# Hybrid decoder trunk: the first projection loaded and used two k at a time, the last output quarter in column halves

## The chip, the cores and the metric
The kernel runs on one core of one Trainium2 chip. The metric is the device time of one launch in microseconds (us). Three runs of the kernel before took 1369.51, 1371.07 and 1371.03 us; the median is 1371.03.

## What is computed
The reference is a four-layer decoder trunk on an input of 256 tokens by 1024 features, all float32. Layers 0 and 3 mix tokens by retention, layer 1 by block-sparse attention, layer 2 by differential attention; each layer ends with a squared-ReLU MLP.

```python
for i in range(DEPTH):                       # 4 layers
    h = _rmsnorm(x, norm1[i])
    m = mixer(h)                             # i % 3: retention, MoBA, differential
    x = x + m
    x = x + _squared_relu_mlp(_rmsnorm(x, norm2[i]), w_up[i], w_down[i])

def _retention_mixer(h, w_in, w_out):        # 4 heads, keys of 256, values of 512
    q, k, v, g = split(h @ w_in)
    q = _rotary(q);  k = _rotary(k) * dk ** -0.5
    s_in = (q @ k.T) * inner_decay
    ...                                      # s_in @ v, normed, gated by silu(g), @ w_out
```

## The kernel before
Every large matrix product is made of float32 parts split in two: a value is rounded to `hi` (ScalarE copies it into the type fp32r) and the rest is `lo` (VectorE subtracts). Three matmuls make one product (`passes`, L296 to L299): hi x hi (L297), hi x lo (L298) and lo x hi (L299). The labels in the trace sort the operand names; for the query and key projections L299 is the matmul that reads `wlo`.

Weights are streamed through three 1 MB buffers `raw`, filled by SP's DMA queue in the order of the list `specs`. Each `raw` is cut into two pieces. For each piece ScalarE writes `whi` (L164) and VectorE writes `wlo` (L174). `advance` (L179) issues these splits up to four pieces ahead of the piece in use, `take` hands a piece to the matmuls, and when the second piece of a buffer has been split, the DMA that refills the buffer is issued (`load_raw`, L134).

The schedule is written out by hand: every engine executes its instructions in the order in which the program issues them. `later(n, fn)` puts a step off by n ticks, and `tick()`, called between groups of matmuls, issues what is due.

The beginning. SP loads x in four blocks of 256 KB with the first weights in between (L202 to L211). ScalarE's queue loads the identity matrix `ident` and the norm weights `rows`, POOL's the small tables (L213 to L220). `norm_quarter` (L266) turns x: two TensorE transposes into one PSUM bank (L272), two ScalarE operations that scale by the norm weight and write `xhi` (L275), two VectorE operations that write `xlo` (L278). The first half of the features (k = 0 to 3) is turned before the first matmul, and the first piece of weights is split; the second half is turned at the first tick, after the matmuls of k = 0 to 2 (`mm_a`, L301, with `first_of_phase`). `rms` (due at tick 3) computes the row norms with two ScalarE squares over x (L284), a POOL operation and VectorE's reciprocal (L289). The row norm itself is applied later, to results.

In `retention`, head 0 makes its query part (w = 0) and its key part (w = 1), each with 48 matmuls of 256 columns into one bank, two pieces each. After each, `rotary` (L417) runs four VectorE operations that read the bank and the cosine table `kd` (L413). Then come the value and gate projections with 512 columns (`vg`).

The end. `finish` (L348) closes the last MLP product by quarters of x, with nine matmuls of 512 columns for each: VectorE scales the bank and adds it to x (L362) and SP stores the quarter (L364).

Of the kernel before, what the change touches and what calls it, by code (L numbers as in the profile page):

```python
# [16 lines left out]
P = 128  # L17
# [14 lines left out]
def trunk(ctx, tc, x_in, rel_bias, norm1, norm2, w_up, w_down, ret_w_in, ret_w_out,  # L32
# [24 lines left out]
    def aux_bank(name):  # L57
        return pa.tile([P, 512], F32, tag="aux", name=name)
# [7 lines left out]
    def later(n, fn, *a):  # L66
        clock[1] += 1
        pending.append((clock[0] + n, ORDER.get(fn.__name__, 3), clock[1], fn, a))
# [62 lines left out]
    raws, pieces = {}, {}  # L131
    nxt = [0, 0, 0, 0]

    def load_raw(half=None):  # L134
        i = nxt[0]
        if i >= len(specs):
            return
        src, a, b = specs[i]
        if half != 1:
            raws[i] = rp.tile([P, a, b], F32, tag="raw", name="raw", bufs=NRAW)  # L140
        if half is None:
            nc.sync.dma_start(raws[i], src)
        else:
            hs = slice(half * (a // 2), (half + 1) * (a // 2))
            nc.sync.dma_start(raws[i][:, hs, :], src[:, hs, :])
        if half != 0:
            nxt[0] += 1

    def parts(i, n):
        m = n if i else n // 2  # L150
        return [slice(c, c + m) for c in range(0, n, m)]

    def split_piece():
        i = nxt[1]
        r = i // 2
        if r >= len(specs):
            return
        nxt[1] += 1
        _, a, b = specs[r]
        half = raws[r][:, (i % 2) * (a // 2):(i % 2 + 1) * (a // 2), :]  # L160
        hi = wp.tile([P, a // 2, b], F32R, tag="hi", name="whi", bufs=NPC)
        lo = wp.tile([P, a // 2, b], F32R, tag="lo", name="wlo", bufs=NPC)
        for part in parts(i, a // 2):
            ACT.activation(hi[:, part], half[:, part], AF.Copy)  # L164
        pieces[i] = (hi, lo, half)
# [31 lines left out]
    X = const.tile([P, 2, D], F32, name="X")  # L197
    xf = x_in.rearrange("b s d -> (b s) d")
    warm = const.tile([P, 1], F32, name="warm")
    DVE.memset(warm, 0.0)  # L200
    ACT.dma_start(ident, c_ident)
    nc.sync.dma_start(X[:, 0, 0:512], xf[0:P, 0:512])  # L202
    ACT.dma_start(rows, norm1.rearrange("l (c p) -> (l c) p", p=P))
    nc.sync.dma_start(X[:, 1, 0:512], xf[P:S, 0:512])
    ACT.activation(warm, warm, AF.Copy)
    load_raw(0)
    for t in range(2):
        nc.sync.dma_start(X[:, t, 512:D], xf[t * P:(t + 1) * P, 512:D])
    load_raw(1)
    for _ in range(1, NRAW):  # L210
        load_raw()  # L211
    rb = const.tile([NB_REL, AH], F32, name="rb")
    POOL.dma_start(rb, rel_bias)  # L213
    rows2 = mp.tile([64, P], F32, tag="t2k", name="rows2", bufs=4)
    POOL.memset(rows2, 0.0)
    POOL.dma_start(rows2[0:32, :], norm2.rearrange("l (c p) -> (l c) p", p=P))
    for i, w in enumerate((moba_q_norm, moba_k_norm, diff_q_norm, diff_k_norm)):
        for g in range(2):
            POOL.dma_start(rows2[32 + i:33 + i, g * HD:(g + 1) * HD], w)
    POOL.dma_start(rows2[36:37, :], diff_subln)  # L220

    W = const.tile([P, 96], F32, name="W")
    wps = aux_bank("wps")
# [21 lines left out]
    def rsqrt(y, v, name, eng):  # L245
        t = small(name + "_t", list(v.shape))
        eng.tensor_scalar(y.bitcast(I32), v.bitcast(I32), -0.5, 1597463007.0, op0=OP.mult, op1=OP.add)
        for _ in range(3):
# [4 lines left out]
            else:  # L253
                eng.tensor_tensor(t, t, v, op=OP.mult)
                eng.tensor_scalar(t, t, -0.5, 1.5, op0=OP.mult, op1=OP.add)
                eng.tensor_tensor(y, t, y, op=OP.mult)

    junk = const.tile([P, D], mybir.dt.bfloat16, name="junk")

    st = {}  # L260

# [4 lines left out]
    def norm_quarter(l, which, c, t):  # L266
        tt = slice(t * P, (t + 1) * P)
        for pair in range(2):
            ps = aux_bank("xt")
            for i in range(2):  # L270
                k = c * 4 + pair * 2 + i
                PE.transpose(ps[:, i * P:(i + 1) * P], X[:, t, k * P:(k + 1) * P], ident)  # L272
            for i in range(2):
                k = c * 4 + pair * 2 + i
                ACT.activation(st["hi"][:, k, tt], ps[:, i * P:(i + 1) * P], AF.Copy, scale=wn(l, which, k))  # L275
            for i in range(2):
                k = c * 4 + pair * 2 + i
                DVE.scalar_tensor_tensor(st["lo"][:, k, tt], ps[:, i * P:(i + 1) * P], wn(l, which, k),  # L278
                                         st["hi"][:, k, tt].bitcast(F32), op0=OP.mult, op1=OP.subtract)
# [21 lines left out]
    def mm_a(ps, half, first_of_phase=False):  # L301
        if not first_of_phase:
            advance()
        hi, lo = take()
        for m in range(2):
            for kk in range(4):
                k = half * 4 + kk
                passes(ps[:, m * S:(m + 1) * S], hi[:, kk, m * P:(m + 1) * P], lo[:, kk, m * P:(m + 1) * P],
                       st["hi"][:, k, :], st["lo"][:, k, :],
                       half == 0 and m == 0 and kk == 0, half == 1 and m == 1 and kk == 3)  # L310
                if first_of_phase and m == 0 and kk == 2:
                    tick()
        tick()

    def mm_b(pst, q, first_of_phase=False):
        if not first_of_phase:
            advance()
        hi, lo = take()
        for kk in range(2):
            k = q * 2 + kk  # L320
            for t in range(2):
                tt = slice(t * P, (t + 1) * P)
                passes(pst[t], st["hi"][:, k, tt], st["lo"][:, k, tt], hi[:, kk, :], lo[:, kk, :],
                       q == 0 and kk == 0, q == 3 and kk == 1)
            if first_of_phase and kk == 0:
                tick()
# [14 lines left out]
    def out_piece(src, first):  # L341
# [3 lines left out]
            mm_o(q, pc, src, first, False)  # L345
        tick()

    def finish(srcs, r2, nxt_norm):  # L348
        advance(4, 4)
        pcs = [take() for _ in srcs]  # L350
        if nxt_norm is not None:
            norm_new()
        for q in QUARTERS:
            for i, (pc, src) in enumerate(zip(pcs, srcs)):
                mm_o(q, pc, src, False, i == len(srcs) - 1)
            c, t = q
            xs = X[:, t, c * 512:(c + 1) * 512]
            ps = st["acc"][q]
            if r2 is None:
                DVE.tensor_tensor(xs, ps, xs, op=OP.add)  # L360
            else:
                DVE.scalar_tensor_tensor(xs, ps, r2[:, t:t + 1], xs, op0=OP.mult, op1=OP.add)  # L362
            if nxt_norm is None:
                nc.sync.dma_start(out.rearrange("b s d -> (b s) d")[t * P:(t + 1) * P, c * 512:(c + 1) * 512], xs)  # L364
            else:
                later(2, norm_quarter, nxt_norm[0], nxt_norm[1], c, t)
            tick()
        if nxt_norm is not None:
            later(3, rms, nxt_norm[1])
# [39 lines left out]

    def retention(l):  # L410
        OT = {}
        kd = mp.tile([P, 8, S], F32, tag="kd", name="kd")
        ACT.dma_start(kd[:, 0:6, :], c_rd.rearrange("a p s -> p a s"))  # L413
        cos_b = kd[:, 0:1, :].to_broadcast([P, 2, S])
        sin_b = kd[:, 1:2, :].to_broadcast([P, 2, S])

# [71 lines left out]
        for h in range(RH):  # L488
            e = {}
            qk = up_.tile([P, 4, S], F32, tag="p4k", name="qk", bufs=6)  # L490
            e["qk"] = qk
            for w in range(2):
                ps = aux_bank("qk")
                mm_a(ps, 0, h == 0 and w == 0)
                mm_a(ps, 1)
                rotary(ps, qk[:, 2 * w:2 * w + 2, :])
            later(2, scores, h, e)
            for w in range(2):
                pst = [mm_bank("vg") for _ in range(2)]
                for q in range(4):  # L500
                    mm_b(pst, q)
                    tick()
                if w == 0:
                    vh = up_.tile([P, 2, 512], F32R, tag="p4k", name="vh", bufs=6)
                    vl = up_.tile([P, 2, 512], F32R, tag="p4k", name="vl", bufs=6)
                    for t in range(2):
                        ACT.activation(vh[:, t, :], pst[t], AF.Copy)
                    for t in range(2):
                        DVE.tensor_tensor(vl[:, t, :], pst[t], vh[:, t, :].bitcast(F32), op=OP.subtract)
                    e["v"] = vh, vl  # L510
                    later(1, av, h, e)
                else:
                    gate(h, e, pst)
                    for t in range(2):
                        gated(h, e, t)
                        later(2, to_feat, h, e, t)
# [237 lines left out]


    norm_new()
    for t in range(2):
        norm_quarter(0, 0, 0, t)
    split_piece()
    split_lo()  # L760
    for t in range(2):
        later(1, norm_quarter, 0, 0, 1, t)
    later(1, split_piece)
    later(1, split_lo)
    later(3, rms, 0)
    later(10, head_weights)
    for l in range(DEPTH):
        if l % 3 == 0:
            retention(l)
# [46 lines left out]
```

## Time and profile before
| | |
|---|---|
| runs | 1369.51, 1371.07, 1371.03 us |
| profiled execution | 1369.67 us |
| its span, first to last instruction | 1367.9 us |
| VectorE, ScalarE, POOL busy | 840.8 us (61%), 689.7 us (50%), 107.1 us (8%) |
| moved by DMA | 242.27 MB, mean 177 GB/s |

Of the 40 equal slices of the span the first and the last have the array less than fully busy:

```profile
PE   7999999999999999999999999999999999999998
```

One slice is 34.2 us. Each digit is the busy share in tenths. The profile's clock line shows full speed in all slices, also where the spacing of the matmuls at the very start shows half of it; so the spacing is the better witness there.

### The profile page before, as it was taken

To read this page: it belongs to the slowest core of one execution; us is meant where nothing else is said; L and a number is where in the kernel's file an instruction comes from. 1 tells how busy PE (TensorE), PEld (TensorE's weight loads), DVE (VectorE), ACT (ScalarE), POOL (GpSimd) and SP (SyncE) were. 2 spreads that over 40 slices of the span, in tenths; PEclk is the share of its full clock that TensorE was granted. 3 is DMA by queue.
4 is the path that set the end of the run, shared out by engine and by line. 5 is a ranking of instruction groups with operands and counts; after the bars stand their busy time and mean duration, and the time that the engine had idled before them with its cause. 6 is when DMAs were issued, how large, how long until landed. Compare 5 with 4: busy or idle time off the path is not lost.

```text
span 1367.9 us, 19806 instructions
## 1 busy us (share of the span) xinstructions
PE 1351.8 (99%) x8020; PEld 1188.7 (87%) x8020; DVE 840.8 (61%) x1238; ACT 689.7 (50%) x1063; POOL 107.1 (8%) x314
## 2 busy tenths in 40 slices
PE   7999999999999999999999999999999999999998
PEld 7888889999987779999987789999988888899997
DVE  6766647555568856555578675555667675555554
ACT  5554436444456745444466754444454444544442
POOL 3111100000032000000021200000031011000000
PEclk9999999999999999999999999999999999999999
DMA  8545464555565346555554346555564555465551
GB/s 274 184 155 184 156 214 157 187 187 188 193 206 181 123 124 219 185 185 185 184 172 137 124 154 216 185 185 185 176 206 144 174 185 185 154 215 186 185 184 63
DMA packets 140797, 242.27 MB, mean 177 GB/s; under 512 B 4256, under 2 KB 87920, under 8 KB 140704
## 3 DMA queue, kind: packets, MB, share of 16 engines
q1 hardware_dynamic: 137872, 236.99, 51.5%
q0 software_dynamic: 1072, 2.35, 0.6%
q10 hardware_dynamic: 1760, 1.66, 0.4%
q8 instruction: 63, 1.03, 0.3%
q14 instruction: 30, 0.25, 0.1%
HBM read 239.91 MB, written 1.07 MB: 176 GB/s over the span
## 4 chain that ended last, share of the span: by engine, by line
PE 97%; ACT 1%; DMA 0%; DVE 0%; issue 0%; SPq 0%; ACTq 0%; DVEq 0%
PE acc L297 12%; PE acc L298 12%; PE acc L299 12%; PE up L299 9%; PE up L298 9%; PE up L297 9%; PE vg L297 4%; PE vg L299 4%; PE vg L298 4%; PE qkv L297 3%; PE qkv L299 3%; PE qkv L298 3%; PE qk L299 2%; PE qk L297 2%; PE qk L298 2%; PE xt L272 1%
## 5 line engine op out<-in xcount | busy, mean ns | idle before, releaser
L174 DVE TENSOR_TENSOR wlo<-raw,whi 128x1024 fp32r<-128x1024 f32 (+1 forms) x449 | 529.5, 1219 | 108.1 <-ACT whi L164 105.8
L164 ACT ACTIVATE whi<-raw 128x1024 fp32r<-128x1024 f32 (+1 forms) x449 | 451.9, 1051 | 90.8 <-PE acc L299 66.8
L297 PE MATMUL up<-xhi,whi 128*128 128x256 f32 x1024 | 290.1, 283 | 0.0
L299 PE MATMUL up<-xhi,wlo 128*128 128x256 f32 x1024 | 289.8, 283 | 0.0
L298 PE MATMUL up<-xlo,whi 128*128 128x256 f32 x1024 | 289.7, 283 | 0.0
L297 PE MATMUL acc<-whi,uu 128*128 128x512 f32 x512 | 200.5, 392 | 0.0
L298 PE MATMUL acc<-wlo,uu 128*128 128x512 f32 x512 | 199.9, 390 | 0.0
L299 PE MATMUL acc<-whi,uu 128*128 128x512 f32 x512 | 199.3, 389 | 0.0
L298 PEld LDWEIGHTS up<-xlo,whi 128*128 128x128 f32 x1024 | 196.3, 192 | 2.2
L297 PEld LDWEIGHTS up<-xhi,whi 128*128 128x128 f32 x1024 | 196.3, 192 | 2.2
L299 PEld LDWEIGHTS up<-xhi,wlo 128*128 128x128 f32 x1024 | 196.3, 192 | 0.0
L378 DVE SCALAR_TENSOR_TENSOR u<-up,u 128x512 f32<-128x512 f32 x64 | 44.2, 691 | 221.7 <-ACT u L377 221.5
L377 ACT ACTIVATE u<-up 128x512 f32<-128x512 f32 x64 | 38.1, 596 | 258.9 <-PE up L299 258.9
L299 PEld LDWEIGHTS acc<-whi,uu 128*128 128x128 f32 x512 | 96.1, 188 | 20.5
L297 PEld LDWEIGHTS acc<-whi,uu 128*128 128x128 f32 x512 | 96.4, 188 | 18.2
L298 PEld LDWEIGHTS acc<-wlo,uu 128*128 128x128 f32 x512 | 96.4, 188 | 17.6
L297 PE MATMUL vg<-whi,xhi 128*128 128x512 f32 x256 | 100.6, 393 | 0.0
L299 PE MATMUL vg<-whi,xlo 128*128 128x512 f32 x256 | 99.8, 390 | 0.0
L298 PE MATMUL vg<-wlo,xhi 128*128 128x512 f32 x256 | 99.7, 390 | 0.0
L297 PE MATMUL qkv<-whi,xhi 128*128 128x512 f32 x192 | 78.0, 406 | 0.0
L297 PE MATMUL acc<-whi,oh 128*128 128x512 f32 x192 | 76.4, 398 | 0.0
L297 PE MATMUL qk<-xhi,whi 128*128 128x256 f32 x256 | 74.0, 289 | 1.8 <-ACT whi L164 1.8
(212 smaller groups left out, 1807.7 us busy)
## 6 DMA issues: line engine op xcount, KB each, us to landing
raw<-in_w_up_dram SPq DMA_DIRECT2D x64, 1024.0 KB, 5.5
raw<-in_w_down_dram SPq DMA_DIRECT2D x64, 1024.0 KB, 5.9
raw<-in_ret_w_in_dram SPq DMA_DIRECT2D x47, 1024.0 KB, 5.2
raw<-in_ret_w_out_dram SPq DMA_DIRECT2D x16, 1024.0 KB, 4.9
raw<-in_moba_w_in_dram SPq DMA_DIRECT2D x12, 1024.0 KB, 5.2
raw<-in_diff_w_in_dram SPq DMA_DIRECT2D x12, 1024.0 KB, 5.1
raw<-in_moba_w_out_dram SPq DMA_DIRECT2D x4, 1024.0 KB, 4.8
raw<-in_diff_w_out_dram SPq DMA_DIRECT2D x4, 1024.0 KB, 4.7
```

The lines of the kernel that those rows point to most:

```text
L164: ACT.activation(hi[:, part], half[:, part], AF.Copy)
L174: DVE.tensor_tensor(lo[:, part], half[:, part], hi[:, part].bitcast(F32), op=OP.subtract)
L272: PE.transpose(ps[:, i * P:(i + 1) * P], X[:, t, k * P:(k + 1) * P], ident)
L297: PE.matmul(ps, lhsT=ah, rhs=bh, start=first, stop=False, skip_group_check=True)
L298: PE.matmul(ps, lhsT=ah, rhs=bl, start=False, stop=False, skip_group_check=True)
L299: PE.matmul(ps, lhsT=al, rhs=bh, start=False, stop=last, skip_group_check=True)
L377: ACT.activation(u, ps, AF.Relu)
L378: DVE.scalar_tensor_tensor(u, ps, 0.0, u, op0=OP.max, op1=OP.mult)
```

## The change
At the beginning, `load_raw` takes a part number, so that a 1 MB weight buffer is loaded in quarters (two k each) or halves. x is loaded in column blocks of 256, in turn with the quarters of the first weights; its first block comes half from SP's queue and half from ScalarE's. The cosine table of layer 0 (`kd0`) comes on SP's queue in two parts. Nine matmuls of bf16 zeros (`hot`) are issued on TensorE ahead of everything else, on a tile that VectorE sets to zero first. A new function `first_qk` makes the query part of head 0: `arrive(pr)` turns two k of x and splits two k of weights, and is called for the next pair after the matmuls of each even k. `rms` comes due at its third tick (k = 7). Pieces 2 and 3 are split in two steps each, as only piece 0 was. POOL's small loads move to tick 4, the head weights to tick 14.

At the end, `last_quarter` makes the last quarter as two blocks of 256 columns, each with its own matmuls, VectorE operation and store.

```diff
-    def load_raw(half=None):
+    def load_raw(part=0, of=1):
...
+        hs = slice(part * (a // of), (part + 1) * (a // of))
+        nc.sync.dma_start(raws[i][:, hs, :], src[:, hs, :])
+        if part == of - 1:
             nxt[0] += 1
...
     def parts(i, n):
-        m = n if i else n // 2
+        m = n if i > 3 else n // 2
...
+    junk = const.tile([P, D], mybir.dt.bfloat16, name="junk")
+    kd0 = mp.tile([P, 8, S], F32, tag="kd", name="kd")
+    DVE.memset(junk, 0.0)
     DVE.memset(warm, 0.0)
+    nc.sync.dma_start(X[:, 0, 0:S], xf[0:P, 0:S])
     ACT.dma_start(ident, c_ident)
+    load_raw(0, 4)
+    ACT.dma_start(X[:, 1, 0:S], xf[P:S, 0:S])
     ACT.dma_start(rows, norm1.rearrange("l (c p) -> (l c) p", p=P))
     ACT.activation(warm, warm, AF.Copy)
+    for i in range(1, 4):
+        nc.sync.dma_start(X[:, :, i * S:(i + 1) * S], xv[:, :, i * S:(i + 1) * S])
+        load_raw(i, 4)
+    load_raw(0, 2)
+    nc.sync.dma_start(kd0[:, 0:2, :], rd[:, 0:2, :])
+    load_raw(1, 2)
+    for i in range(2):
+        load_raw(i, 2)
+    nc.sync.dma_start(kd0[:, 2:6, :], rd[:, 2:6, :])
+    hot = aux_bank("hot")
+    for _ in range(9):
+        PE.matmul(hot, lhsT=junk[:, :P], rhs=junk[:, :512], start=True, stop=True)
...
+    def first_qk(ps):
...
+        def arrive(pr):
+            bank = aux_bank("xt")
+            for i in range(2):
+                for t in range(2):
+                    c0 = i * S + t * P
+                    k = 2 * pr + i
+                    PE.transpose(bank[:, c0:c0 + P], X[:, t, k * P:(k + 1) * P], ident)
+            for i in range(2):
+                k = 2 * pr + i
+                ACT.activation(st["hi"][:, k, :], bank[:, i * S:(i + 1) * S], AF.Copy, scale=wn(0, 0, k))
+            for i in range(2):
+                k = 2 * pr + i
+                DVE.scalar_tensor_tensor(st["lo"][:, k, :], bank[:, i * S:(i + 1) * S], wn(0, 0, k),
+                                         st["hi"][:, k, :].bitcast(F32), op0=OP.mult, op1=OP.subtract)
+            hi, lo = pieces[pr // 2]
+            kk = slice(pr % 2 * 2, pr % 2 * 2 + 2)
+            raw = raws[0][:, 2 * pr:2 * pr + 2, :]
+            ACT.activation(hi[:, kk], raw, AF.Copy)
+            DVE.tensor_tensor(lo[:, kk], raw, hi[:, kk].bitcast(F32), op=OP.subtract)
+
+        arrive(0)
+        for k in range(KC):
...
+            for m in range(2):
+                mc = slice(m * P, (m + 1) * P)
+                passes(ps[:, m * S:(m + 1) * S], hi[:, kk, mc], lo[:, kk, mc], st["hi"][:, k, :], st["lo"][:, k, :],
+                       k == 0 and m == 0, k == KC - 1 and m == 1)
+            if k % 2 == 0 and k < KC - 2:
+                arrive(k // 2 + 1)
+            if k in (3, 5, 7):
+                tick()
+        nxt[1] = nxt[2] = nxt[3] = 2
...
+        load_raw()
...
+    def last_quarter(pcs, srcs, r2):
+        for e in range(2):
+            cc = slice(512 + e * S, 512 + (e + 1) * S)
+            ps = st["acc"][1, 1][:, e * S:(e + 1) * S]
+            for i, ((hi, lo), (uh, ul)) in enumerate(zip(pcs, srcs)):
+                passes(ps, uh[:, P:S], ul[:, P:S], hi[:, 0, cc], lo[:, 0, cc], False, e == 1 and i == len(srcs) - 1)
+            xs = X[:, 1, cc]
+            DVE.scalar_tensor_tensor(xs, ps, r2[:, 1:2], xs, op0=OP.mult, op1=OP.add)
+            nc.sync.dma_start(out.rearrange("b s d -> (b s) d")[P:S, cc], xs)
...
-                mm_a(ps, 0, h == 0 and w == 0)
-                mm_a(ps, 1)
+                if l == 0 and h == 0 and w == 0:
+                    first_qk(ps)
+                else:
+                    mm_a(ps, 0, h == 0 and w == 0)
+                    mm_a(ps, 1)
...
-    for t in range(2):
-        norm_quarter(0, 0, 0, t)
-    split_piece()
-    split_lo()
-    for t in range(2):
-        later(1, norm_quarter, 0, 0, 1, t)
-    later(1, split_piece)
-    later(1, split_lo)
     later(3, rms, 0)
-    later(10, head_weights)
+    later(4, small_loads)
+    later(14, head_weights)
```

## Rows read from the trace of the kernel before

**Rows 1.** Page, part 1: engine, busy time, share of the span, instructions.
```profile
PE 1351.8 (99%) x8020; PEld 1188.7 (87%) x8020; DVE 840.8 (61%) x1238; ACT 689.7 (50%) x1063; POOL 107.1 (8%) x314
```

**Rows 2.** Timeline, TensorE, 8.8 to 20 us: start, length, engine, line, operation.
```profile
8.89 0.58 PE L297 MATMUL qk<-xhi,whi 128*128 128x256 f32 x1 [1.83 <-ACT whi L164]
...
9.99 0.42 PE L297 MATMUL qk<-xhi,whi 128*128 128x256 f32 x1
10.21 0.42 PE L298 MATMUL qk<-xlo,whi 128*128 128x256 f32 x1
...
15.04 0.30 PE L297 MATMUL qk<-xhi,whi 128*128 128x256 f32 x1
...
15.41 0.28 PE L297 MATMUL qk<-xhi,whi 128*128 128x256 f32 x1
...
16.88 0.39 PE L299 MATMUL qk<-xhi,wlo 128*128 128x256 f32 x1 [0.36 <-DVE wlo L174]
17.11 0.28 PE L297 MATMUL qk<-xhi,whi 128*128 128x256 f32 x1
...
19.85 0.28 PE L299 MATMUL qk<-xhi,wlo 128*128 128x256 f32 x1
```

**Rows 3.** Timeline, ScalarE, 5.8 to 9 us.
```profile
5.81 0.63 ACT L275 ACTIVATE xhi<-xt,W 128x128 fp32r<-128x128 f32 x2 [2.65 <-PE xt L272]
...
8.21 0.63 ACT L164 ACTIVATE whi<-raw 128x512 fp32r<-128x512 f32 x1 [0.22 <-DMA raw<-in_ret_w_in_dram]
...
8.74 0.62 ACT L164 ACTIVATE whi<-raw 128x512 fp32r<-128x512 f32 x1
```

**Rows 4.** Timeline, VectorE, 0 to 10 us.
```profile
0.81 0.06 DVE L200 MEMSET warm<- 128x1 f32 x1 [0.81 <-PEq L804]
...
6.47 0.35 DVE L278 SCALAR_TENSOR_TENSOR xlo<-xt,W,xhi 128x128 fp32r<-128x128 f32 x1 [1.09 <-ACT xhi L275]
...
8.87 1.29 DVE L174 TENSOR_TENSOR wlo<-raw,whi 128x512 fp32r<-128x512 f32 x2 [0.23 <-ACT whi L164]
```

**Rows 5.** Timeline, ScalarE and VectorE, 21 to 26.1 us: row norm, then rotary.
```profile
21.33 1.05 ACT L284 ACTIVATE junk<-X 128x1024 bf16<-128x1024 f32 x1
...
23.97 0.17 DVE L289 RECIPROCAL r<-me 128x2 f32<-128x2 f32 x1 [1.09 <-POOL me L286]
24.05 0.69 DVE L421 TENSOR_TENSOR ra<-qk,kd 128x512 f32<-128x512 f32 x1
...
26.05 2.36 DVE L174 TENSOR_TENSOR wlo<-raw,whi 128x1024 fp32r<-128x1024 f32 x2
```

**Rows 6.** Timelines at 774 and 777 us; last row by line: duration ns min/median/max.
```profile
774.10 0.84 ACT L734 ACTIVATE oh<-oT,qsc 128x256 fp32r<-128x256 f32 x2
...
777.12 0.87 DVE L735 SCALAR_TENSOR_TENSOR ol<-oT,qsc,oh 128x256 fp32r<-128x256 f32 x2
...
L735 DVE SCALAR_TENSOR_TENSOR ol<-oT,qsc,oh x8: 476/478/484, 777.1 to 794.8; 128x256 fp32r<-128x256 f32 x8
```

**Rows 7.** Timeline, 56.6 to 57.5 us: transposes and ScalarE's read of them.
```profile
56.81 0.93 PE L481 MATMUL oT<-ident,go 128*128 128x128 f32 x7
57.44 0.60 ACT L485 ACTIVATE oh<-oT 128x512 fp32r<-128x512 f32 x1 [2.37 <-PE oT L481]
```

**Rows 8.** DMA issues, first 40 us: count, KB each, median us to landing.
```profile
raw<-in_ret_w_in_dram SPq DMA_DIRECT2D x2, 512.0 KB, 7.5
...
rows<-in_norm_dram ACTq DMA_DIRECT2D x1, 16.0 KB, 3.5
```

**Rows 9.** Timelines from 1363 us; last row: busy times of a stretch, GB/s last.
```profile
1363.01 0.39 PE L298 MATMUL acc<-wlo,uu 128*128 128x512 f32 x1
1363.23 0.39 PE L299 MATMUL acc<-whi,uu 128*128 128x512 f32 x1
...
1363.66 0.75 DVE L362 SCALAR_TENSOR_TENSOR X<-acc,r,X 128x512 f32<-128x512 f32 x1 [1.29 <-PE acc L299]
...
1365.40:1366.10 0.70, 0.00 (x0) 0.00 (x0) 0.00 (x0) 0.00 (x0) 0.00 (x0) 1.00 0.82 310
```

More of the change, by code (lines that the diff above doesn't have):

```diff
@@ L138, in load_raw @@
         src, a, b = specs[i]
-        if half != 1:
+        if part == 0:
             raws[i] = rp.tile([P, a, b], F32, tag="raw", name="raw", bufs=NRAW)
[L141 to L146, printed above, removed]
+        hs = slice(part * (a // of), (part + 1) * (a // of))
+        nc.sync.dma_start(raws[i][:, hs, :], src[:, hs, :])
+        if part == of - 1:
             nxt[0] += 1
     def parts(i, n):
-        m = n if i else n // 2
+        m = n if i > 3 else n // 2
         return [slice(c, c + m) for c in range(0, n, m)]
@@ L199, in trunk, with small_loads @@
     warm = const.tile([P, 1], F32, name="warm")
+    junk = const.tile([P, D], mybir.dt.bfloat16, name="junk")
+    kd0 = mp.tile([P, 8, S], F32, tag="kd", name="kd")
+    rd = c_rd.rearrange("a p s -> p a s")
+    DVE.memset(junk, 0.0)
     DVE.memset(warm, 0.0)
+    xv = xf.rearrange("(t p) d -> p t d", p=P)
+    nc.sync.dma_start(X[:, 0, 0:S], xf[0:P, 0:S])
     ACT.dma_start(ident, c_ident)
-    nc.sync.dma_start(X[:, 0, 0:512], xf[0:P, 0:512])
+    load_raw(0, 4)
+    ACT.dma_start(X[:, 1, 0:S], xf[P:S, 0:S])
     ACT.dma_start(rows, norm1.rearrange("l (c p) -> (l c) p", p=P))
-    nc.sync.dma_start(X[:, 1, 0:512], xf[P:S, 0:512])
     ACT.activation(warm, warm, AF.Copy)
-    load_raw(0)
-    for t in range(2):
[L208 to L211, printed above, removed]
+    for i in range(1, 4):
[10 more added lines that the diff above has]
+        PE.matmul(hot, lhsT=junk[:, :P], rhs=junk[:, :512], start=True, stop=True)
     rb = const.tile([NB_REL, AH], F32, name="rb")
-    POOL.dma_start(rb, rel_bias)
     rows2 = mp.tile([64, P], F32, tag="t2k", name="rows2", bufs=4)
[L215 to L220, printed above, removed]
+    def small_loads():
+        POOL.dma_start(rb, rel_bias)
+        POOL.memset(rows2, 0.0)
+        POOL.dma_start(rows2[0:32, :], norm2.rearrange("l (c p) -> (l c) p", p=P))
+        for i, w in enumerate((moba_q_norm, moba_k_norm, diff_q_norm, diff_k_norm)):
+            for g in range(2):
+                POOL.dma_start(rows2[32 + i:33 + i, g * HD:(g + 1) * HD], w)
+        POOL.dma_start(rows2[36:37, :], diff_subln)
     W = const.tile([P, 96], F32, name="W")
@@ L256, in rsqrt @@
                 eng.tensor_tensor(y, t, y, op=OP.mult)
-    junk = const.tile([P, D], mybir.dt.bfloat16, name="junk")
     st = {}
@@ L313, in mm_a @@
         tick()
+    def first_qk(ps):
+        for i in range(2):
+            hi = wp.tile([P, 4, S], F32R, tag="hi", name="whi", bufs=NPC)
+            lo = wp.tile([P, 4, S], F32R, tag="lo", name="wlo", bufs=NPC)
+            pieces[i] = (hi, lo)
+        def arrive(pr):
[8 more added lines that the diff above has]
+                ACT.activation(st["hi"][:, k, :], bank[:, i * S:(i + 1) * S], AF.Copy, scale=wn(0, 0, k))
+            for i in range(2):
+                k = 2 * pr + i
[8 more added lines that the diff above has]
+        for k in range(KC):
+            hi, lo = pieces[k // 4]
+            kk = k % 4
+            for m in range(2):
[7 more added lines that the diff above has]
+        nxt[1] = nxt[2] = nxt[3] = 2
+        for i in range(2):
+            pieces.pop(i)
+        load_raw()
     def mm_b(pst, q, first_of_phase=False):
@@ L353, in finish @@
         for q in QUARTERS:
+            c, t = q
+            if nxt_norm is None and q == QUARTERS[-1]:
+                last_quarter(pcs, srcs, r2)
+                return
             for i, (pc, src) in enumerate(zip(pcs, srcs)):
                 mm_o(q, pc, src, False, i == len(srcs) - 1)
-            c, t = q
             xs = X[:, t, c * 512:(c + 1) * 512]
@@ L411, in retention @@
         OT = {}
-        kd = mp.tile([P, 8, S], F32, tag="kd", name="kd")
-        ACT.dma_start(kd[:, 0:6, :], c_rd.rearrange("a p s -> p a s"))
+        if l == 0:
+            kd = kd0
+        else:
+            kd = mp.tile([P, 8, S], F32, tag="kd", name="kd")
+            ACT.dma_start(kd[:, 0:6, :], rd)
         cos_b = kd[:, 0:1, :].to_broadcast([P, 2, S])
@@ L493, in retention @@
                 ps = aux_bank("qk")
-                mm_a(ps, 0, h == 0 and w == 0)
-                mm_a(ps, 1)
+                if l == 0 and h == 0 and w == 0:
+                    first_qk(ps)
+                else:
+                    mm_a(ps, 0, h == 0 and w == 0)
+                    mm_a(ps, 1)
                 rotary(ps, qk[:, 2 * w:2 * w + 2, :])
@@ L756, in trunk @@
     norm_new()
-    for t in range(2):
-        norm_quarter(0, 0, 0, t)
-    split_piece()
-    split_lo()
-    for t in range(2):
-        later(1, norm_quarter, 0, 0, 1, t)
-    later(1, split_piece)
-    later(1, split_lo)
     later(3, rms, 0)
-    later(10, head_weights)
+    later(4, small_loads)
+    later(14, head_weights)
     for l in range(DEPTH):
```

## The prediction
> **What bounds the kernel now.** I read the page's engine table first: TensorE is busy for 99% of the span [rows 1], so a change of the two ends can move the time only by what TensorE loses there. The second view is TensorE's own timeline of the beginning [rows 2]. The reader is to see three things in it. The first 256-column matmuls follow each other every 0.21 us (9.99 to 10.21), which is 1.2 GHz; from 15.04 on they follow every 0.12 us (three steps from 15.04 to 15.41), which is the 2.4 GHz level. After a wait the next matmul comes 0.22 us later instead of 0.12 (16.88, 17.11). And the second half of head 0 (w = 1) has its third matmul, the first that reads a `wlo`, at 19.85, without a wait. From there to the end the array runs nearly gapless, so that point is my yardstick: whatever the changed kernel does before it counts by when this same matmul can start. The third view is the timelines of ScalarE and VectorE in that stretch [rows 3 to 5], for the durations and for who waits for whom. The tail is read last [rows 8, 9].
>
> **Warm-up and first pair.** VectorE's first memset is at 0.81 [rows 4]. The new one (128x1024, bf16) has no row: it lies between nothing and 1.2 us, two float passes of 512 columns at 0.60 us each (x2 in 1.29, the last lasting 0.69) [rows 4]; I take half of that, 0.6, for half the bytes. The nine zero matmuls, 512 columns wide, cost twice 0.2135 us each at the low clock, 3.84 us, and end at 5.3. The Trainium skill, "VectorE: DVE Perf Modes", section "Zero memsets can be issued as uint32 (trn2)", says that a memset takes one cycle per element whatever its type, and that a zero one can be issued on four-byte words. By its 0.96 GHz in "Trainium Kernel Development and Optimization" (Hardware Hierarchy) I estimate 1.07 us, or 0.53 as words; no row here shows a wide memset. By the first the sum below would grow by 0.5. The norm weights (`rows`) took 3.5 us to land [rows 8] and are now issued one DMA later (0.45 us) with 128 KB of x ahead; about 5.2. So the small transpose runs at 5.3 and the first of the four x transposes one slot later, at 5.5; the fourth is done at 5.5 + 3 x 0.2135 + 0.42 = 6.56.
>
> **The chain of one pair.** `arrive` puts these behind each other: four transposes, two `xhi` on ScalarE, `whi` on ScalarE; on VectorE two `xlo`, then `wlo`; the even k's third matmul reads `wlo`. The old rows show that the first `xlo` waited for the second `xhi` (5.81 + 0.63 = 6.44, start 6.47) [rows 3, 4], and ScalarE for the whole group of transposes. I take both over. From the first transpose: 0.64 to ScalarE's start at the high clock (56.81 to 57.44) [rows 7]; two 128x256 `xhi` from PSUM, 0.84 (0.36 to the second's start and 0.48) [rows 6]; 0.03 to VectorE; two `xlo` at 0.395 (the form of L735: two in 0.87, one 0.48) [rows 6] = 0.79; `wlo` 0.69 [rows 4]; 0.05 to TensorE. Together 3.04. `whi` (0.72 + 0.63 behind the first `xhi`) is done before and costs nothing. So the first `wlo` matmul runs at 6.56 + 0.04 + 0.84 + 0.03 + 0.79 + 0.69 + 0.05 = 9.0.
>
> **The wait that this makes.** The transposes of the next pair stand behind all six matmuls of the even k in TensorE's order, and only the odd k (6 x 0.12 = 0.7 us) stands between them and the next even k. So the next chain starts at 9.0 + 0.22 + 3 x 0.12 = 9.58, and one pair costs 3.04 + 0.58 = 3.62 us, of which TensorE has work for 1.9 (12 x 0.12 and 4 x 0.11). The three later pairs start at 9.58, 13.20 and 16.82; the last even k gets its `wlo` matmul at 19.86, k = 7 follows at 20.44, and w = 1 could begin at 21.15, its predecessors finished at 21.32.
>
> **What is queued behind that.** Formerly the pieces up to number 5 were split ahead; now none is. Behind the last `whi` ScalarE has `rms` (the tick at k = 7), and VectorE has the reciprocal and the four rotary operations before the first `wlo` of piece 2. The last `whi` starts at 16.82 + 0.64 + 0.72 = 18.18 and lets `rms` start 0.53 later [rows 3], at 18.71; from the first square to the reciprocal is 2.64 (21.33 to 23.97) [rows 5]: 21.35. Rotary starts 0.08 later, at 21.43, just after its matmuls end, and takes 2.00 (24.05 to 26.05) [rows 5]; the half `wlo` of piece 2 takes 0.69: 24.12. The yardstick matmul runs at 24.17 instead of 19.85: 4.3 us later, and the slow first slot after a wait adds 0.1. Start: **+4.4 us**. Bounds: if both groupings of the chain fall away (first `xlo` behind the first `xhi`, ScalarE behind two transposes), a pair costs 0.5 less and the start is +2.9; if the low clock holds through the stage, see the second rival.
>
> **Edits that I cost at nothing.** x and weights in quarters: the 512 KB pieces took 7.5 us to land [rows 8]; the last quarter is issued at about 4.5 and so lands by about 12, while its `whi` could not start before 18.18; if that cover were gone the stage would stretch by the excess. The third weight reload waits for the last `wlo` (19.8) instead of 16.9 and is hidden behind the four pieces ahead of it; the cosine table moves from ScalarE's queue to SP's, ten issues deep, and is needed only at 21.4. The small loads leave POOL's start for the fourth tick and stand there behind the `rms` chain; the head weights move from tick 10 to 14 with them, some 30 us behind the loads. If they were late the array would wait once for a few us; nothing in the rows suggests it. Splitting pieces 2 and 3 in halves adds an instruction of about 0.1 us to each of two engines, and saves 0.5 of the wait above, which is counted.
>
> **The end.** Nine 512-column matmuls (0.227 us apart [rows 9]: 2.04) become eighteen of 256 (0.118: 2.12), +0.08; the last VectorE operation shrinks from 0.75 [rows 9] to 0.48 [rows 6], -0.27; the last store from 256 to 128 KB. 256 KB at 310 GB/s [rows 9] are 0.85 us, so the half saves at most 0.42 and at least nothing; I take 0.35. End: **-0.5 us**. The first half's store is issued 0.9 us before and hides beside the second's matmuls.
>
> **Sum.** +4.4 - 0.5 = +3.9 us. The profiled execution took 1369.67 us, 1.8 around its span of 1367.9; it becomes 1373.6. The median of the runs shown, 1371.03, is 1.4 above that execution, and would become 1374.9; of four executions two stand at either level, and I forecast 1374.5.
>
> **Rivals.** *The pairs overlap (not slower).* If the next transposes did pass the waiting matmul, or the chain were shorter than I read it, a pair would cost TensorE's own 1.9 us: the stage would end 5.2 earlier, at 16.0, rms and rotary would still hold the yardstick back to about 19.0, and the time would be 1.4 below before: about 1369.6. It decides below a pair of about 2.3 us, where the start breaks even with the tail (3 x 1.3 saved). For it: the old kernel's transposes stood behind matmuls too, and it lost little. Against: in the old rows TensorE at 16.88 let nothing past the waiting matmul.
>
> *The low clock holds.* The zeros run at 1.2 GHz and the array is then half idle; the old start kept the low level until 15.04 although it was busy most of the time from 8.89. At 0.2135 a slot, a pair costs 3.50 + 1.02 = 4.5 and the yardstick slips to about 28; w = 1's 46 matmuls then cost up to 0.095 more each. That is +8 to +12: about 1380. The pause of 2.6 us before the yardstick could also send the clock down, for +2 or so. For it: pauses. Against: 5 us without a gap precede the stage.
>
> *The groupings fall away.* Start +2.9, time 1373.0. For it: TensorE and the other engines signal each instruction elsewhere (rotary's single steps wait for each other). Against: rows 3 and 4.
>
> *The loads are late.* The Trainium skill, "DMA: Bandwidth & Descriptors", section "Rules for kernel authors", asks for at least 1 MiB per DMA for full bandwidth, which speaks against quarters. As a mechanism here: a quarter would have to land 6 us later than 12 to matter, and each us beyond adds one, say 1377. The rows' 7.5 us for a half speak against it.
>
> **How the numbers follow.** Forecast 0.50 (1373 to 1376), low clock 0.20, groupings 0.18, overlap 0.10, late loads 0.02. A difference under 0.2% (2.7 us) is no change that can be told here: between 1368.3 and 1373.8. Of the forecast about a third of its chance (0.15), of the groupings most (0.13) and of the overlap 0.05 fall in it: same 0.33. Faster: the other half of the overlap, 0.05. Slower: the rest, 0.62. The range leaves out the overlap below and the worst of the low clock above: 1371.0 to 1380.5.
>
> **What would show it.** Right: transposes `xt` in four groups 3.6 us apart with TensorE idle before the even k's third matmul, released by `wlo`; another pause of about 2.6 us before the first `wlo` matmul of w = 1, with reciprocal, rotary and the half `wlo` in one row on VectorE; the first `vg` matmul near 29.8 instead of 25.4; a last VectorE operation of 0.48. Wrong: groups closer than 2.3 us, or a start at which w = 1 runs straight on. The clock rival shows as 0.21 us between matmuls after 9 us.

## Result and profile after

The changed kernel took 1377.09 us (median; 1376.59 to 1378.69), the kernel before 1370.92 in the same comparison: ratio 1.0052, 95% interval 1.0039 to 1.0064. It is 6.2 us slower; 1374.5 was forecast. The profiled execution took 1377.23 us, 7.56 more than the one before, and the account below is made on these two.

The page's engine line answers to [rows 1]: the array's busy time grew by 5.5 us, with the same products and 18 more matmuls (nine of zeros, which take 4.0 us, and nine from the last quarter, whose 18 are half as wide).

```profile
span 1375.5 us, 19854 instructions
PE 1357.3 (99%) x8038; PEld 1190.8 (87%) x8038; DVE 840.5 (61%) x1235; ACT 688.9 (50%) x1058; POOL 108.2 (8%) x314
```

TensorE's timeline of the beginning, the answer to [rows 2] (L309 to L311 are the former L297 to L299, L222 are the zeros, L340 is the transpose in `arrive`; in brackets stands how long the engine had been idle and what released it):

```profile
1.45 4.02 PE L222 MATMUL hot<-junk 128*128 128x512 bf16 x9 [1.45 <-DVE warm L201]
6.47 0.22 PE L238 MATMUL wps<-ident,rows 32*128 32x32 f32 x1 [0.99 <-DMA rows<-in_norm_dram]
6.62 0.66 PE L340 MATMUL xt<-ident,X 128*128 128x128 f32 x4
...
9.71 0.58 PE L311 MATMUL qk<-xhi,wlo 128*128 128x256 f32 x1 [0.26 <-DVE wlo L352]
...
10.74 1.05 PE L340 MATMUL xt<-ident,X 128*128 128x128 f32 x4
...
14.23 0.39 PE L311 MATMUL qk<-xhi,wlo 128*128 128x256 f32 x1 [0.49 <-DVE wlo L352]
...
17.85 0.39 PE L311 MATMUL qk<-xhi,wlo 128*128 128x256 f32 x1 [0.49 <-DVE wlo L352]
...
21.47 0.39 PE L311 MATMUL qk<-xhi,wlo 128*128 128x256 f32 x1 [0.49 <-DVE wlo L352]
...
25.77 0.51 PE L311 MATMUL qk<-xhi,wlo 128*128 128x256 f32 x1 [2.06 <-DVE wlo L171]
26.08 0.42 PE L309 MATMUL qk<-xhi,whi 128*128 128x256 f32 x1
26.30 0.42 PE L310 MATMUL qk<-xlo,whi 128*128 128x256 f32 x1
...
32.88 0.40 PE L309 MATMUL vg<-whi,xhi 128*128 128x512 f32 x1
```

The reader is to see the ladder 14.23, 17.85, 21.47: one pair of k every 3.62 us, each time released by `wlo`. Then 25.77, the yardstick, which stood at 19.85 [rows 2]; the idle time before it is put down to the `wlo` of piece 2. And after it 0.22 us between matmuls: the low clock again. The first `vg` matmul stands at 32.88, in the kernel before at 25.37:

```profile
25.37 0.40 PE L297 MATMUL vg<-whi,xhi 128*128 128x512 f32 x1
```

So 7.5 of the 7.6 us that the span grew (1367.9 to 1375.5) are lost ahead of this matmul. VectorE shows why that `wlo` was late:

```profile
22.95 0.17 DVE L301 RECIPROCAL r<-me 128x2 f32<-128x2 f32 x1 [1.54 <-POOL me L298]
23.04 0.69 DVE L494 TENSOR_TENSOR ra<-qk,kd 128x512 f32<-128x512 f32 x1
...
25.04 7.03 DVE L171 TENSOR_TENSOR wlo<-raw,whi 128x512 fp32r<-128x512 f32 x8
```

Reciprocal, rotary, and only then the split of the pieces that the array waits for. The clock in five stretches (busy time and count of each engine, then the granted clock, DMA share, GB/s):

```profile
5.41:8.81 3.40, 0.96 (x7) 0.65 (x6) 0.82 (x3) 1.36 (x3) 0.00 (x0) 1.00 1.07 359
8.82:12.22 3.40, 3.15 (x13) 2.85 (x14) 0.84 (x2) 0.39 (x2) 0.00 (x0) 0.50 1.08 352
12.24:25.87 13.63, 7.84 (x51) 6.21 (x50) 7.30 (x16) 9.07 (x19) 2.40 (x10) 1.00 0.61 205
25.89:29.28 3.39, 3.39 (x16) 3.39 (x17) 3.39 (x5) 2.74 (x3) 3.06 (x5) 0.50 0.24 25
29.31:33.00 3.69, 3.69 (x32) 3.69 (x32) 2.76 (x3) 0.00 (x0) 3.39 (x7) 1.00 0.99 366
```

1.00 is the 2.4 GHz level, 0.50 the 1.2 GHz one. The zeros had raised the clock before the first transposes: the four at 6.62 take 0.66 us, the four at 10.74, at 0.50, take 1.05. It fell at 8.8, after a stretch in which the array was busy for 0.96 us of 3.40, and again at 25.9, after the pause before the yardstick. With all its slots taken, the array ran 16 matmuls in the stretch from 25.89 and 32 in the slightly longer one after.

The tail, the answer to [rows 9]:

```profile
1368.92 0.28 PE L309 MATMUL acc<-whi,uu 128*128 128x256 f32 x1
...
1370.19 0.48 DVE L412 SCALAR_TENSOR_TENSOR X<-acc,r,X 128x256 f32<-128x256 f32 x1 [0.32 <-PE acc L311]
...
1370.72 0.39 PE L309 MATMUL acc<-whi,uu 128*128 128x256 f32 x1 [0.58 <-DVE X L412]
...
1372.09 0.48 DVE L412 SCALAR_TENSOR_TENSOR X<-acc,r,X 128x256 f32<-128x256 f32 x1 [1.42 <-PE acc L311]
```

In the kernel before, the quarter's first matmul was this one:

```profile
1361.42 0.39 PE L297 MATMUL acc<-whi,uu 128*128 128x512 f32 x1
```

The first matmul of the second half waits 0.58 us until VectorE has read the first half, which lies in the same PSUM bank; whether the bank or the program's own bookkeeping of that tile makes it wait was not tried. From the last VectorE operation's start to the span's end it is now 3.4 us instead of 4.2, but that start comes 0.9 us later behind the quarter's first matmul (3.17 instead of 2.24).

### The profile page after: what moved, and what is told of

It reads as the page before. It is cut to its first block, busy times and chain, and to the rows that moved or that the text cites. A ratio compares the mean times of both kernels' runs of the same rounds, so it can differ in the third digit from the quotient of the medians.

```text
span 1375.5 us, 19854 instructions
## 1 busy us (share of the span) xinstructions
PE 1357.3 (99%) x8038; PEld 1190.8 (87%) x8038; DVE 840.5 (61%) x1235; ACT 688.9 (50%) x1058; POOL 108.2 (8%) x314
## 4 chain that ended last, share of the span: by engine, by line
PE 97%; ACT 2%; DVE 1%; issue 0%; DMA 0%; ACTq 0%; POOL 0%; DVEq 0%
PE acc L309 12%; PE acc L310 12%; PE acc L311 12%; PE up L311 9%; PE up L310 9%; PE up L309 9%; PE vg L309 4%; PE vg L311 4%; PE vg L310 4%; PE qkv L309 3%; PE qkv L311 3%; PE qkv L310 3%; PE qk L311 2%; PE qk L309 2%; PE qk L310 2%; PE xt L284 1%
## 5 line engine op out<-in xcount | busy, mean ns | idle before, releaser
L309 PE MATMUL up<-xhi,whi 128*128 128x256 f32 x1024 | 290.1, 283 | 0.0
L311 PE MATMUL up<-xhi,wlo 128*128 128x256 f32 x1024 | 289.8, 283 | 0.0
L309 PE MATMUL acc<-whi,uu 128*128 128x512 f32 (+1 forms) x515 | 201.2, 391 | 0.6 <-DVE X L412 0.6
L310 PE MATMUL acc<-wlo,uu 128*128 128x512 f32 (+1 forms) x515 | 200.4, 389 | 0.0
L311 PE MATMUL acc<-whi,uu 128*128 128x512 f32 (+1 forms) x515 | 199.8, 388 | 0.0
L309 PEld LDWEIGHTS up<-xhi,whi 128*128 128x128 f32 x1024 | 196.3, 192 | 2.2
L311 PEld LDWEIGHTS up<-xhi,wlo 128*128 128x128 f32 x1024 | 196.3, 192 | 0.0
L311 PEld LDWEIGHTS acc<-whi,uu 128*128 128x128 f32 x515 | 96.7, 188 | 20.5
L309 PEld LDWEIGHTS acc<-whi,uu 128*128 128x128 f32 x515 | 97.0, 188 | 18.7 <-DVE X L412 0.8
L309 PE MATMUL vg<-whi,xhi 128*128 128x512 f32 x256 | 100.5, 393 | 0.0
L311 PE MATMUL vg<-whi,xlo 128*128 128x512 f32 x256 | 99.8, 390 | 0.0
L309 PE MATMUL qk<-xhi,whi 128*128 128x256 f32 x256 | 75.0, 293 | 3.7 <-ACT whi L351 3.4
L309 PE MATMUL qkv<-whi,xhi 128*128 128x512 f32 x192 | 78.0, 407 | 0.0
L311 PE MATMUL qk<-xhi,wlo 128*128 128x256 f32 x256 | 74.1, 289 | 3.8 <-DVE wlo L171 2.1
```

Source lines behind the costliest of these rows:

```text
L309: PE.matmul(ps, lhsT=ah, rhs=bh, start=first, stop=False, skip_group_check=True)
L310: PE.matmul(ps, lhsT=ah, rhs=bl, start=False, stop=False, skip_group_check=True)
L311: PE.matmul(ps, lhsT=al, rhs=bh, start=False, stop=last, skip_group_check=True)
```

## Experiments

Theory: the order of the work (pairs behind matmuls, nothing split ahead) and the clock that falls in its pauses made the change slow. Rivals: late loads; the clock alone; VectorE as the bound. All times are medians beside the kernel before on the same chip (1370.3); the changed kernel itself (1377.09 us) was not run again beside them.

**The two ends apart.** The changed kernel with the old last quarter:

```diff
-            if nxt_norm is None and q == QUARTERS[-1]:
-                last_quarter(pcs, srcs, r2)
-                return
```

> The changed kernel with the old last quarter (nine matmuls of 512 columns, one store). In the changed kernel's trace the second column half's first matmul waited 0.58 us for VectorE to finish the first half, which eats the gain of the shorter last operation and store. Theory 'the halves cost what they save': same as the changed kernel within 0.2 us, 1377.0, last quarter's first matmul to the span's end 6.5 us. Rival, the prediction's own term: the halves save 0.5 us, so 1377.6 here.

Measured 1378.65 us (1378.13 to 1379.29), ratio 1.0062 (1.0049 to 1.0074), which overlaps the changed kernel's. Both expectations, 1377.0 and 1377.6, were missed by a microsecond or more, so the time decides nothing between them. In the profiled execution (1378.19) the reason is elsewhere: near 773 us the array ran at half clock for 3.4 us, which the changed kernel's profile does not have, and from the first `vg` to the end it took 1.3 us longer (32.50 to 1376.4 against 32.88 to 1375.5). The last section returns to this. And the kernel before with the new last quarter alone (the same lines added, and `last_quarter`):

> The kernel before with only the last quarter in column halves. Theory 'the halves cost what they save': 1371.0, with a wait of about 0.6 us of TensorE for VectorE (X) in the last quarter. Rival, the prediction's term: 0.5 us faster than before, 1370.4.

Measured 1370.19 us against 1370.34, ratio 1.0000 (0.9991 to 1.0009). The same wait is there (first row: us in total, times, longest); the two rows below it are the last quarter's first matmul in this kernel and in the changed one with the old quarter:

```profile
PE acc L297 <- DVE X L356: 0.6, 1, 0.6
...
1362.72 0.28 PE L297 MATMUL acc<-whi,uu 128*128 128x256 f32 x1
...
1370.03 0.39 PE L309 MATMUL acc<-whi,uu 128*128 128x512 f32 x1
```

From the last quarter's first matmul to the span's end it is 6.6 us in the changed kernel (1368.92 to 1375.5) and 6.4 with its old quarter (1370.03 to 1376.4); it is 6.5 us with the halves alone (1362.72 to 1369.2) and 6.5 in the kernel before (1361.42 to 1367.9). The interval of the time alone (1.2 us either way) would not exclude 0.5; with the rows it goes against the prediction's term. The loss is the start's.

**Zeros in the pauses.** `keep(n)` issues n zero matmuls of 128x512 from a tile of zeros of their own.

```diff
-    for _ in range(9):
+    for _ in range(12):
...
         arrive(0)
+        keep(4)
         for k in range(KC):
...
         load_raw()
+        keep(10)
```

> The changed kernel with more zero matmuls (128x512, bf16, from a tile of their own): 12 instead of 9 at the start, 4 between the first transposes and k = 0, and 10 between the query and the key part, all meant to fall into TensorE's pauses. Theory 'order and clock': the order's waits stay (pairs 3.6 us apart, key part's first wlo matmul about 4 us later than before), but the clock does not fall: the first pair costs 0.9 less and the key part 1.6 less, 2.5 together, 1374.6. If the clock has no part in it: 1377.1 or above. If only the clock made the change slow: near 1371.

Measured 1375.00 us (1374.84 to 1375.23), ratio 1.0035. The clock stays up over the whole stage, the ladder keeps its 3.62 us, and the yardstick comes at 24.86:

```profile
24.86 0.38 PE L319 MATMUL qk<-xhi,wlo 128*128 128x256 f32 x1 [0.45 <-DVE wlo L171]
...
6.20:26.00 19.80, 14.60 (x92) 10.80 (x91) 10.00 (x22) 11.60 (x22) 3.35 (x11) 1.00 0.75 250
```

So the clock is worth about 2 us of the 6 (2.1 between the medians, which come from two comparisons, 2.4 between the profiled spans, 1375.5 and 1373.1), and what is left is the order's waits: the array was kept fed with zeros, not with work.

**Pieces split ahead.** The new lines stand right behind `arrive(3)`, the last pair's.

```diff
+            if k == 4:
+                nxt[1] = nxt[3] = 2
+                for _ in range(2):
+                    split_piece()
+                    split_lo()
...
-        nxt[1] = nxt[2] = nxt[3] = 2
+        nxt[2] = 2
```

> The changed kernel with the weight pieces 2 and 3 split right after the last pair's operations, ahead of row norm and rotary on ScalarE and VectorE. Theory 'order and clock': the pause of 2.9 us before the key part's first wlo matmul goes, and the fall of the clock behind it (1.6 us) with it: 1372.7; the pairs stay 3.6 us apart. Rival 'late loads': the second weight buffer isn't there yet (it landed at 12 to 14 us in the changed kernel), and little changes: above 1376.

Measured 1374.66 us (1373.11 to 1376.09), ratio 1.0032 (1.0020 to 1.0045). The pause is gone: four `wlo` in a row now stand ahead of rotary, and the key part runs straight on.

```profile
22.60 2.49 DVE L171 TENSOR_TENSOR wlo<-raw,whi 128x512 fp32r<-128x512 f32 x4
26.30 0.17 DVE L301 RECIPROCAL r<-me 128x2 f32<-128x2 f32 x1 [1.21 <-POOL me L298]
...
24.03 0.28 PE L309 MATMUL qk<-xhi,whi 128*128 128x256 f32 x1
24.15 0.28 PE L310 MATMUL qk<-xlo,whi 128*128 128x256 f32 x1
24.27 0.28 PE L311 MATMUL qk<-xhi,wlo 128*128 128x256 f32 x1
```

It came out 2 us above what was expected. In the profiled execution (1374.11) the low clock held from 8.1 to 21.7, and the pairs took 4.5 us, not 3.6, the figure of the prediction's second rival; the other five executions have no profile:

```profile
8.07:21.71 13.64, 12.45 (x48) 10.69 (x48) 4.51 (x11) 4.16 (x11) 0.00 (x0) 0.50 0.70 236
```

**Pairs prepared one ahead.**

```diff
         arrive(0)
+        arrive(1)
...
-            if k % 2 == 0 and k < KC - 2:
-                arrive(k // 2 + 1)
+            if k % 2 == 0 and k < KC - 4:
+                arrive(k // 2 + 2)
```

> The changed kernel with each pair of k prepared one pair earlier: pairs 0 and 1 before the first matmul, pair 2 after k = 0, pair 3 after k = 2. Theory 'order and clock': the wait of each pair behind the even k's matmuls goes; the query part ends near 17 to 18.5 us instead of 22.7, the pause before the key part stays (rotary and the half wlo still stand ahead), the key part's first wlo matmul near 21 instead of 25.8; with the clock's fall behind the pause 1372.5. Rival 'late loads': pair 1 is ready no earlier than before, groups of transposes stay more than 3 us apart, above 1375.

Measured 1372.75 us, ratio 1.0014 (1.0006 to 1.0023). The query part's last matmul starts at 18.25, and the pause before the key part is still there, 2.05 us of it behind `wlo`:

```profile
18.82 0.39 PE L309 MATMUL qk<-xhi,whi 128*128 128x256 f32 x1 [0.29 <-ACT whi L161]
19.05 0.28 PE L310 MATMUL qk<-xlo,whi 128*128 128x256 f32 x1
21.38 0.39 PE L311 MATMUL qk<-xhi,wlo 128*128 128x256 f32 x1 [2.05 <-DVE wlo L171]
```

The same loads, in the same order, now serve a stage whose yardstick comes 4.4 us earlier (21.38), so the loads were not late. The changed kernel's trace says the same: its 256 KB quarters of weights landed 4.9 us after their issue (median), the prediction had reckoned with 7.5, and none of the `whi` in the stage waited for a DMA.

**Both, with the old last quarter.** The edits of the last two experiments and of the first, together.

> Pairs prepared one earlier and pieces 2 and 3 split ahead of row norm and rotary, with the old last quarter. Theory 'order and clock': neither wait is left, the key part's first wlo matmul comes at 17 to 18 us, 2 to 3 us earlier than in the kernel before, and the array isn't idle long enough to fall: 1368. Rival: VectorE, which now has 4 x 1.5 us for the pairs and 2.4 us for the pieces in a row, is the bound, and the point comes at 19 to 20: 1370, as before.

Measured 1368.38 us, ratio 0.9985 (0.9976 to 0.9994): faster than both kernels, and 1.9 us below the one before. The yardstick comes at 18.84, and TensorE's list of waits over the first 30 us holds, behind the first transposes, only two short ones:

```profile
18.84 0.28 PE L311 MATMUL qk<-xhi,wlo 128*128 128x256 f32 x1
...
PE qk L309 <- ACT whi L351: 0.6, 1, 0.6
PE qk L311 <- DVE wlo L352: 0.2, 1, 0.2
```

The yardstick is later than the 17 to 18 that were expected and close to the rival's 19. But VectorE still idles, for 1.65 us before the third pair's `xlo` and 1.04 us before the fourth's, while the array's matmuls stand 0.21 us apart, the spacing of the low clock, until 13.6. The last experiment has the same work on VectorE, the high clock and the yardstick at 16.59; so VectorE was not the bound here.

**Without the zeros.**

```diff
-    for _ in range(9):
+    for _ in range(0):
         PE.matmul(hot, lhsT=junk[:, :P], rhs=junk[:, :512], start=True, stop=True)
```

> The changed kernel without the nine zero matmuls at the start. Theory 'order and clock': the pairs run at the low clock (4.5 us each instead of 3.6) for longer, and the key part's first wlo matmul comes 1 to 3 us later: 1378 to 1380. Rival 'zeros bring nothing, since the clock falls again at 8.8 us': as the changed kernel, 1377.

Measured 1377.22 us (1376.58 to 1380.56), ratio 1.0063 (1.0049 to 1.0077): as the changed kernel, so the theory's 1 to 3 us failed. In its profile the pairs ran at 4.5 us until the clock rose at 18.5, and the yardstick came 0.8 later than in the changed kernel; but the clock did not fall in the pause before it, where the changed kernel lost 1.6 us (the matmuls behind it stand 0.12 us apart):

```profile
26.57 0.39 PE L311 MATMUL qk<-xhi,wlo 128*128 128x256 f32 x1 [2.05 <-DVE wlo L171]
26.79 0.28 PE L309 MATMUL qk<-xhi,whi 128*128 128x256 f32 x1
26.91 0.28 PE L310 MATMUL qk<-xlo,whi 128*128 128x256 f32 x1
```

So the rival's time came true, but not its reason alone: the zeros brought the yardstick 0.8 us forward, and the fall behind it took that back. The profiled execution is the fastest of the five (1376.58), the others were not looked at; why the clock falls in that pause in one execution and not in the other was not tried.

**Both, with zeros that last.** Eleven zeros at the start, four behind the first transposes, and the norm weights' DMA ahead of the second x block:

> The kernel both_ahead with 11 zero matmuls at the start instead of 9, 4 more between the first transposes and k = 0, and the norm weights' DMA ahead of the second x block on ScalarE's queue. Theory 'order and clock': the first matmuls run at the high clock and the first transposes start 0.5 to 1 us earlier: 1367. Rival: the clock is high by then anyway and the zeros that run over delay the first pair: as both_ahead or 0.5 us slower.

Measured 1367.95 us, ratio 0.9984 (0.9976 to 0.9993). In its profile the clock is high from 5.8 through the whole stage and the yardstick stands at 16.59, 3.3 us ahead of the kernel before:

```profile
16.59 0.28 PE L319 MATMUL qk<-xhi,wlo 128*128 128x256 f32 x1
...
5.80:25.00 19.20, 18.48 (x132) 16.36 (x131) 14.26 (x26) 13.50 (x24) 5.53 (x14) 1.00 0.96 327
```

By its time it can't be told from the one without (1368.38), whose times spread more (1366.47 to 1370.74 against 1366.43 to 1368.69). The two profiles tell more: the first `vg` comes 2.2 us earlier (22.11 against 24.36), but the profiled execution with the lasting zeros has a stretch of half clock near 765 us, which the other has not, and from there to the end it takes 1.8 us longer (22.11 to 1366.2 against 24.36 to 1366.6).

## Why the prediction was right, and what it mis-sized

The direction and the mechanism held: pairs 3.6 us apart released by `wlo`, the pause ahead of the yardstick with reciprocal, rotary and the half `wlo` in one row, the last operation of 0.48. Only the first `vg` matmul stands at 32.9 instead of 29.8. The range held the time too, but 1377.1 lies above the 1373 to 1376 of the forecast itself, and it is inside the range only because room was left for the clock; the sign of that rival, 0.21 us between matmuls, came as well, in two stretches. By its steps, on the two profiled executions (+3.9 forecast, +7.6 measured):

- *The chain of one pair* was 3.62 us and is 3.62 (17.85 to 21.47). The groupings hold (the first `xlo` starts 0.03 us behind the second `xhi`, ScalarE behind all four transposes), so that rival is out; so is the overlap, which would have needed the order that was tried as pairs_ahead.
- *What is queued behind* was 4.31 from the last pair's `wlo` matmul to the yardstick and is 4.30 (21.47 to 25.77).
- *Warm-up and first pair* was 9.0 and is 9.71. The memset was near: issued as 128x512 uint32 it took 0.48 us, where the sum has 0.6. The Trainium skill's four-byte form ("VectorE: DVE Perf Modes", "Zero memsets can be issued as uint32 (trn2)") is what the trace shows, and 0.53 had been estimated from it (the 0.96 GHz stands in "Trainium Kernel Development and Optimization" under NeuronCore Architecture). What was short is the norm weights' landing: 4.7 us after their issue at 1.67, not 3.5, so the array stood idle for 0.99 us and the first transposes started at 6.62, not 5.5: +1.1. Against it, they were costed at the low clock and ran at the high one: ScalarE started 0.69 us behind the first of them, not 1.1: -0.4. Together +0.7, less than the landing's error alone.
- *The clock* was mis-sized: the forecast let it stay up, and the rival let it stay down through the whole stage. The "against" of that rival counted 5 us without a gap; the zeros are 3.84 in the prediction's own sum and 4.02 in the trace, and what they raised did not last. (Its yardstick of 28 is too late by its own terms as well: 24.17 and three pairs at 0.9 more make 26.9. no_zeros, low until 18.5, has 26.57.) The clock did something between: it fell after the zeros and made the first pair 4.52 us (9.71 to 14.23), +0.9; it fell in the pause, which the rival had named as a possibility at +2 or so, and made yardstick to `vg` 7.11 us instead of 5.52, of which 0.1 had been counted, +1.5.
- *The end* was -0.5 and is +0.1. The shorter last operation and store are there (0.8 us), and the wait between the halves takes them back. The step that failed is the one in which eighteen matmuls follow each other without a gap; +0.6.

Together 0.7 + 0.9 + 1.5 + 0.6 = 3.7, the difference of 7.6 and 3.9. The medians are only 2.6 apart (1377.1 measured, 1374.5 forecast), since the forecast put the median 0.9 above the profiled execution and it came out level with it (1377.09, 1377.23); that part is luck. The edits costed at nothing (quarters, late third reload, cosine table, small loads) were free: no wait in TensorE's list after the yardstick is new, but the tail's.

## What to carry to other kernels

Before cutting a load finer, write down what stands in each engine's order between the arrival and the use: here each pair's preparation stood behind the previous pair's use, and a step that had been run four pieces ahead was run none ahead. Preparation goes one stage before use, and post-processing (rotary, row norm) behind the splits that the array waits for. Warm-up work has to last until the real work arrives, and no pause may follow: here nine zeros that ended a microsecond before it left the time where it was (1377.1 us with them, 1377.2 without), and zeros that also filled the pauses gave about 2 us.

## What was not expected of the hardware

The clock can also fall in the middle of the kernel, in one execution and not in another. In the profile of the tail_only kernel a stretch near 767 us ran at half clock, in the kernel before the same stretch did not:

```profile
767.27:770.66 3.39, 3.39 (x9) 2.67 (x8) 3.25 (x15) 3.39 (x10) 0.78 (x3) 0.50 0.00 0
```

```profile
767.27:770.66 3.39, 3.39 (x16) 2.81 (x16) 3.25 (x17) 3.26 (x11) 0.78 (x3) 1.00 0.02 5
```

Between these two profiles the time from the first `vg` to the end is 1.5 us longer with the dip (25.18 to 1369.2 against 25.37 to 1367.9). Three of the ten profiles have it, tail_only, start_only and both_ahead_zeros. In each it begins within 1.5 us of the end of the same wait, the 1.5 us that TensorE's `sc` matmuls there wait for VectorE's `nm`; the other seven have that wait too, and no fall. The 27 times of the kernel before split the same way: the 13 from 1369.1 to 1369.9 us have a mean granted clock of 0.999 or 1.000, and of the 14 from 1370.3 to 1371.8 all but one have 0.998, where 3.4 us at half clock would take 0.0012 off the mean. So the two levels of its times are probably executions without and with the dip. It has the size of the smaller differences in this document, so two kernels are best compared by the rows up to the first `vg` as well as by the time.

The profile's granted clock reads 1.00 for everything ahead of the first recorded change: in no_zeros it stands at 1.00 up to 18.5 us, while the pairs ran at 4.5 us, as they did at 0.50 in split_ahead. There the spacing of the matmuls is the witness.
